# Position vectors as a bias row in the compression, GELU behind the transposes, and three query tiles split at full width and placed by DMA, in a hybrid attention block on Trainium2

## The chip, the cores and the metric

The kernel runs on one core of one Trainium2 chip (trn2). The metric is the device time of one launch in microseconds (us), lower is better. Before the change three timed runs gave 637.34, 634.45 and 636.11 us, with a median of 636.11 us. TensorE multiplies matrices, VectorE (DVE in the profile) and ScalarE (ACT) work element by element, GpSimd (POOL) does the same more slowly, and SyncE (SP) issues every DMA transfer, in order, from one queue.

## The reference, cut to what matters

The block has 512 tokens of width 1024. One input projection feeds a sparse attention group of 8 query heads in 2 key/value groups and a short convolution group; an output projection and a gated MLP follow. The part that the change touches is the compression of keys and values: windows of 32 tokens, one every 16 tokens (31 windows), get a position vector added to each token, go through a hidden layer of 256 with GELU, and become one compressed key or value each.

```python
def compress_kv(kv, pe, w1, w2):
    n_cmp = (S - L_CMP) // S_CMP + 1                       # 31
    idx = jnp.arange(n_cmp)[:, None] * S_CMP + jnp.arange(L_CMP)[None, :]
    blk = kv[:, idx] + pe[None, None, :, None, :]
    blk = blk.transpose(0, 3, 1, 2, 4).reshape(B, G, n_cmp, L_CMP * dh)
    return jax.nn.gelu(blk @ w1, approximate=True) @ w2
```

The queries are scaled by 1/8 and multiplied with compressed, selected and sliding-window keys. With these shapes the selected and the sliding branch both see all causal keys.

## The kernel before, in words

Every float32 operand is split into hi (the leading 12 bits, made by ScalarE as a copy into the type fp32r) and lo (the rest, made by VectorE as a subtraction). A projection is then three TensorE products per contraction tile of 128: weight hi with activation hi (L167), weight hi with activation lo (L168), weight lo with activation hi (L169), each 128x512. Weights come through `Stream`: SyncE loads a tile into one of 3 raw buffers (L72), ScalarE makes its hi part (L84), VectorE its lo part (L85; GpSimd for the eight tiles `w_c` of the compression's hidden layer), into a ring of 4 tiles. A raw buffer is loaded again when its lo part has been made.

The order of work: value and gate columns first; then the projections k0, k1 (keys), c0 (keys to compress), q0, q1 (queries of heads 0 to 3); then the attention, tile of 128 queries by tile, last tile first, with the remaining products as fillers between its pieces. The fillers are listed in `ORDER`: c1 (values to compress), q2, q3, the hidden layer h0 to h7, the second layer s, and then the convolution's products g, x, b. A scheduler (the tile framework) fixes the instruction order of each engine at build time by priorities; on the chip each engine then runs its own list in order, and an instruction whose operand is late holds all that stand behind it.

What the change touches:

- `queries(qa, p)` (L390 to L399) takes the projection `p` of two heads, multiplies it by the inverse norm (`normed`, L372, VectorE) into `qt`, and splits it head by head into `Q2`: ScalarE writes hi for 64 partitions (L397), VectorE writes lo into the other 64 partitions (L398). This is four instructions of 64x512 per query tile.
- `blocks(kv, p)` (L407 to L420) normalizes c0 or c1 into `ct`, and adds the position vectors `peT` while it gathers the windows: eight VectorE additions of 64x248 (L417) into two tiles `x`, each of which is then split into `X` (L420: ScalarE hi, VectorE lo, 128x496). The hidden layer's products `ph` (L441) take `X` as the stationary operand; one window slot of 32 in each group is a spare, set to zero.
- `second_layer()` (L445 to L472) adds the hi and lo rows of `ph` into `g1` (L450, L451), takes the GELU of them on ScalarE (L452), transposes (`pg`, L455), copies to `GT` and `GV` (L459, L461), and makes the compressed keys `KC` (L464 to L466, with a DMA that copies them to the other 64 partitions) and values `VC`.

The attention's scores are `sc` (L593); VectorE adds the bias and takes the minimum (L597, tile `P`), ScalarE the exponential (L599), VectorE makes the scale (`sums`, L604, L606), ScalarE (L613) or GpSimd (L611, the first head) multiplies by it, TensorE transposes (`tr`, L622), the result is split into `pth` and `ptl` (two buffers each, L131 and L132 in `split`), and multiplied with V into `o` (L630, L631). The compressed scores are `pcs` (L547).

Of the kernel before, what the change touches and what calls it, by code (L numbers as in the profile page):

```python
# [21 lines left out]
F32 = mybir.dt.float32  # L22
F32R = mybir.dt.float32r
# [7 lines left out]
NT = S // P          # token tiles  # L31
KT = D // P          # contraction tiles of the model width
# [9 lines left out]
# the projections and the first layer of the compression as they fill the gaps of the attention:  # L42
# values to compress c1, queries q, hidden layer h, second layer s, then gate g, input x, output gate b
# [3 lines left out]
T_TILES = 20         # kc vc ks kw q0-3 then (c x b) x 4  # L47
WARM = 8             # products on zeros while the first loads are under way


def f32(ap):
    return ap.bitcast(F32)


class Stream:
    """The dense weights in the order of their use: loaded some tiles ahead, split fewer ahead."""

    def __init__(self, tc, nc, raw, ring, items, loads=3, splits=2):
        self.tc, self.nc, self.raw, self.ring, self.items = tc, nc, raw, ring, items
        self.loads, self.splits = loads, splits  # L60
        self.raws, self.tiles = [], []
        self.at = 0
        self.early = False     # whether the splits go before what was emitted shortly before them
        self.pool_lo = set()  # tiles whose lo part GpSimd makes
        self.pieces = {}     # tiles that are split in pieces of so many columns
        self.other = {}      # tiles that go to another pool than the ring
# [41 lines left out]
def block_kernel(ctx: ExitStack, tc: tile.TileContext, a, out):  # L108
# [20 lines left out]
    def split(hi, lo, src):  # L129
        """hi = src rounded to 12 significant bits, lo = src - hi (exact)."""  # L130
        act(hi, src, AF.Copy)  # L131
        nc.vector.tensor_tensor(lo, src, f32(hi), op=ALU.subtract)  # L132

    VK = [0, 2, 5, KT]       # the k tiles of the value columns, as they share a tile of the ring
# [58 lines left out]
    # the tensor engine's clock comes up while the first loads are under way  # L193
# [6 lines left out]
    # bias tables: U[p, h, u] = -(bias of distance p + 384 - u), +BIG where it is negative  # L200
    # row r of vrows is the whole of vd; reading with a pitch one short shifts it by r
# [46 lines left out]
    def rstd_of(ss, name):  # L248
        """1 / rms of a row from the two halves of its mean square."""
# [21 lines left out]
    # The mean square of a row divides what comes out of the products, not what goes in.  # L271
    R = const.tile([P, 2, NT], F32, name="R")        # 1 / rms and its negative, by token
    Rb = ph1.tile([P, S], F32, name="Rb")            # the same, by token along the row
# [114 lines left out]
    # queries, scaled by -1/8; even heads keep hi in the low half, odd heads in the high half  # L388
    Q2 = r16("Q2", F32R).rearrange("p (h t) -> p h t", h=NH)

    def queries(qa, p):
        p = normed(p, f"qt{qa}")
        for e in range(2):
# [9 lines left out]
    # X[(l parity, d), l // 2, k/v, hi/lo, (group, block)] = kv + pe, the blocks padded to 32  # L403
    X = opool.tile([P, 16, 2, 2, NG, 32], F32R, tag="o16", name="X")
    nc.vector.memset(f32(X[:, :, :, :, :, NCMP:]), 0.0)

    def blocks(kv, p):  # L407
        p = normed(p, f"ct{kv}")
        for lh in range(2):
            x32 = ph1.tile([P, 8, NG, 32], F32, tag="t2", bufs=3, name=f"x32_{kv}_{lh}")  # L410
            for lp in range(2):
                for g in range(NG):
                    src = p[g * HD:(g + 1) * HD, :]
                    v = bass.AP(tensor=src.tensor, offset=src.offset + lp + 16 * lh,
                                ap=[src.ap[0], [2, 8], [16, NCMP]])
                    pev = peT[lp * HD:(lp + 1) * HD, kv, lh * 8:lh * 8 + 8]
                    nc.vector.tensor_tensor(  # L417
                        x32[lp * HD:(lp + 1) * HD, :, g, :NCMP], v,
                        pev[:, :, None].to_broadcast([HD, 8, NCMP]), op=ALU.add)
            ls = slice(lh * 8, lh * 8 + 8)  # L420
            split(X[:, ls, kv, 0, :, :NCMP], X[:, ls, kv, 1, :, :NCMP], x32[:, :, :, :NCMP])
# [7 lines left out]
    def hidden_steps(c):  # L429
        """First layer of the compression; rows 0-63 from X hi, rows 64-127 from X lo."""  # L430
# [3 lines left out]
        for l in range(2):  # L434
            l2 = 2 * c + l
            for kv in range(2):
                xs = X[:, l2, kv].rearrange("p s g n -> p (s g n)")
                for s in range(2):
                    cc = slice(l * 512 + kv * 256, l * 512 + kv * 256 + 256)
                    # one group over the bank: its first product opens it  # L440
# [4 lines left out]
    def second_layer():  # L445
        w2 = ph1.tile([P, 2, 2, HD], F32, tag="gz", bufs=1, name="w2")     # (half, k/v)
# [5 lines left out]
        act(g1[:HD, :S], g1[:HD, :S], AF.Gelu_apprx_tanh)  # L452
# [3 lines left out]
        GT = ph1.tile([P, 2, HD], F32, tag="t2", bufs=3, name="GT")  # L456
        GV = ph1.tile([P, 2, NG, 4, 32], F32, tag="t2", bufs=3, name="GV")
        pgv = pg[:, :256].rearrange("p (v f c) -> p v f c", v=2, f=2)
        nc.vector.tensor_copy(GT, pgv[:, 0])  # L459
        for g in range(NG):  # L460
            nc.vector.tensor_copy(GV[:, :, g], pgv[:, 1, :, None, 32 * g:32 * g + 32].to_broadcast([P, 2, 4, 32]))  # L461
        pc = pt_bank("pc")
        for hf in range(2):
            MM(pc[:HD, :HD], w2[:, hf, 0, :], GT[:, hf, :], start=hf == 0, stop=hf == 1)  # L464
# [109 lines left out]
    class Part:  # L574
        """Four heads of a group on a tile of queries: one branch, or both for the first tile."""
# [76 lines left out]
    def finish(o, i, g):  # L652
        # rows 0-63: V hi . P, rows 64-127: V lo . P
# [23 lines left out]
    for n, (i, g, bs) in enumerate(parts):  # L677
# [6 lines left out]
        # the share that goes between this part's pieces  # L684
# [45 lines left out]
    def token_major(w_tiles, ys, acts, on_half, on_tile, order):  # L730
        """The last products of a streamed contraction, one token tile after another."""
# [206 lines left out]
```

## Time and profile before

| what | value |
|---|---|
| timed runs | 637.34, 634.45, 636.11 us; median 636.11 us |
| span of the profiled execution | 633.9 us (the profile gives no other time for it) |
| TensorE busy | 617.5 us (97% of the span) |
| VectorE busy | 382.2 us (60%) |
| ScalarE busy | 306.5 us (48%) |
| GpSimd busy | 62.7 us (10%) |
| mean granted TensorE clock | 0.995 of full |

The span runs from the first to the last instruction; the lowest timed run is 0.55 us above it, the median 2.2 us. "Busy" is the share of time in which an engine has an instruction under way. Since TensorE is busy for nearly the whole span, a change helps only where it takes away one of TensorE's few waits, and costs where it makes a new one.

### The profile page before, as it was taken

Reading aid. Unit: us, or ns where it says so; the run is one execution under the profiler, and the core shown is the slowest. Engines: PE = TensorE matmul, PEld = TensorE weight load, DVE = VectorE, ACT = ScalarE, POOL = GpSimd, SP = SyncE. Lnnn points to the kernel's source line nnn. Section 1 sums busy time; section 2 is a strip of 40 time slices with the busy share of each in tenths; the row PEclk is TensorE's granted clock in tenths of the full one; section 3 lists DMA queues with packets and bytes.
Section 4 is the critical chain, followed back from the end, with each engine's and each line's share of the span. In section 5 each row is a group of like instructions: output and inputs, shape, how many; then the busy total and the mean of one; then the engine's idle time right before and its main releaser. Section 6 shows DMA issues by size and latency. Waiting matters only on the chain.

```text
span 633.9 us, 8027 instructions
## 1 busy us (share of the span) xinstructions
PE 617.5 (97%) x2980; PEld 511.3 (81%) x2980; DVE 382.2 (60%) x668; ACT 306.5 (48%) x556; POOL 62.7 (10%) x88
## 2 busy tenths in 40 slices
PE   8998899999999999999999999999999999999995
PEld 6886688887778788898888888888888888888884
DVE  5379967898988756648666656565656542222225
ACT  6546765798878644426443434444344422222212
POOL 1102453002130202200000000000000000000001
PEclk9999899999999999999999999999999999999999
DMA  8993355201121483004222233232322232232203
GB/s 293 329 304 129 133 180 189 74 10 43 42 78 53 169 280 130 8 5 143 93 96 98 99 100 101 100 100 99 101 87 95 89 114 87 94 100 99 67 0 133
DMA packets 25302, 72.00 MB, mean 114 GB/s; under 512 B 3136, under 2 KB 7048, under 8 KB 25008
## 3 DMA queue, kind: packets, MB, share of 16 engines
q1 hardware_dynamic: 25264, 71.50, 33.9%
q8 instruction: 23, 0.38, 0.2%
q14 instruction: 15, 0.12, 0.1%
HBM read 67.50 MB, written 4.74 MB: 114 GB/s over the span
## 4 chain that ended last, share of the span: by engine, by line
PE 80%; DVE 10%; DMA 3%; ACT 3%; issue 2%; POOL 1%; SPq 0%; DVEq 0%; POOLq 0%; ACTq 0%
PE pu L168 13%; PE pu L169 13%; PE pu L167 13%; PE z L743 6%; PE z L742 6%; PE z L744 6%; PE y L744 2%; PE y L743 2%; PE y L742 2%; DVE x L417 2%; DMA raw_q<-in_w_t 2%; PE tr L622 2%; PE sc L593 2%; PE o L631 1%; PE o L630 1%
## 5 line engine op out<-in xcount | busy, mean ns | idle before, releaser
L167 PE MATMUL pu<-h2T,w_u 128*128 128x512 f32 (+1 forms) x384 | 142.8, 372 | 0.0
L168 PE MATMUL pu<-h2T,w_u 128*128 128x512 f32 (+1 forms) x384 | 142.7, 372 | 0.0
L169 PE MATMUL pu<-h2T,w_u 128*128 128x512 f32 (+1 forms) x384 | 142.6, 371 | 0.0
L167 PEld LDWEIGHTS pu<-h2T,w_u 128*128 128x128 f32 x384 | 72.3, 188 | 12.6
L168 PEld LDWEIGHTS pu<-h2T,w_u 128*128 128x128 f32 x384 | 72.3, 188 | 12.6 <-DVE h2T L132 0.2
L169 PEld LDWEIGHTS pu<-h2T,w_u 128*128 128x128 f32 x384 | 72.3, 188 | 12.4
L826 DVE SCALAR_TENSOR_TENSOR cv<-pu,ffnw,cv 128x511 f32<-128x511 f32 x44 | 32.9, 749 | 70.2 <-ACT cv L825 70.2
L85 DVE TENSOR_TENSOR w_d<-raw_d,w_d 128x1024 fp32r<-128x1024 f32 x22 | 26.9, 1224 | 72.8 <-ACT w_d L84 72.8
L742 PE MATMUL z<-w_d,aT 128*128 128x512 f32 x176 | 68.5, 389 | 0.0
L743 PE MATMUL z<-w_d,aT 128*128 128x512 f32 x176 | 68.5, 389 | 0.0
L744 PE MATMUL z<-w_d,aT 128*128 128x512 f32 x176 | 68.5, 389 | 0.0
L825 ACT ACTIVATE cv<-pu,ffnw 128x512 f32<-128x512 f32 x44 | 30.3, 688 | 64.0 <-PE pu L169 63.9
L84 ACT ACTIVATE w_d<-raw_d 128x1024 fp32r<-128x1024 f32 x22 | 23.3, 1059 | 75.2 <-PE z L744 75.2
L85 DVE TENSOR_TENSOR w_u<-raw_u,w_u 128x1024 fp32r<-128x1024 f32 x44 | 53.4, 1217 | 5.9 <-ACT w_u L84 5.8
L84 ACT ACTIVATE w_u<-raw_u 128x1024 fp32r<-128x1024 f32 x44 | 46.2, 1052 | 6.6 <-PE pu L169 6.3
L599 ACT ACTIVATE P<-P,mins 128x512 f32<-128x512 f32 (+3 forms) x64 | 35.4, 554 | 11.5 <-DVE mins L597 11.1
L742 PEld LDWEIGHTS z<-w_d,aT 128*128 128x128 f32 x176 | 33.0, 188 | 6.9
L744 PEld LDWEIGHTS z<-w_d,aT 128*128 128x128 f32 x176 | 33.0, 188 | 6.9
L743 PEld LDWEIGHTS z<-w_d,aT 128*128 128x128 f32 x176 | 33.0, 188 | 6.7
L131 ACT ACTIVATE aT<-cv 128x512 fp32r<-128x512 f32 x22 | 13.9, 632 | 49.5 <-DVE cv L843 49.5
L251 POOL TENSOR_SCALAR rsz<-ssz 128x1 f32<-128x1 f32 x4 | 1.2, 300 | 355.2 <-ACT jz L865 355.2
L827 DVE SCALAR_TENSOR_TENSOR cv<-pu,ffnw,cv 128x510 f32<-128x510 f32 x44 | 32.8, 748 | 1.5
(215 smaller groups left out, 1158.7 us busy)
## 6 DMA issues: line engine op xcount, KB each, us to landing
raw_u<-in_w_u SPq DMA_DIRECT2D x44, 512.0 KB, 3.3
raw_d<-in_w_d SPq DMA_DIRECT2D x22, 512.0 KB, 3.2
raw_c<-in_w_c SPq DMA_DIRECT2D x8, 512.0 KB, 3.3
raw_o<-in_w_o SPq DMA_DIRECT2D x8, 512.0 KB, 3.4
vrows<-vd SPq DMA_DIRECT2D x2, 1280.0 KB, 10.4
xT<-in_xT SPq DMA_DIRECT2D x8, 256.0 KB, 5.3
xt<-in_x SPq DMA_DIRECT2D x4, 512.0 KB, 7.1
raw_q<-in_w_t SPq DMA_DIRECT2D x4, 512.0 KB, 7.0
```

The source lines that it names most:

```text
L84: self.nc.scalar.activation(t[:, 0, cs], self.raws[n][:, cs], AF.Copy)
L85: eng.tensor_tensor(t[:, 1, cs], self.raws[n][:, cs], f32(t[:, 0, cs]), op=ALU.subtract)
L167: MM(dst, wh, xh, start=first, stop=False)
L168: MM(dst, wh, xl, start=False, stop=False)
L169: MM(dst, wl, xh, start=False, stop=last)
L599: act(v, v, AF.Exp, bias=m, scale=-1.0, accum_out=self.sums[:, r, b:b + 1])
L742: MM(y, oh_, w[:, 0, cs], start=first, stop=False)
L743: MM(y, ol_, w[:, 0, cs], start=False, stop=False)
L744: MM(y, oh_, w[:, 1, cs], start=False, stop=last)
L825: act(t, pu, AF.Copy, scale=ffnw[:, m, 2:3])
L826: nc.vector.scalar_tensor_tensor(t[:, 1:], pu[:, :S - 1], ffnw[:, m, 1:2], t[:, 1:], op0=ALU.mult, op1=ALU.add)
L827: nc.vector.scalar_tensor_tensor(t[:, 2:], pu[:, :S - 2], ffnw[:, m, 0:1], t[:, 2:], op0=ALU.mult, op1=ALU.add)
```

## The change: what it does

- The position vectors are no longer added to the windows. By linearity they go through the hidden layer on their own: they are split once into the spare window slot of group 0 of `X`, so that their hidden row comes out of the same products; behind the transposes it is a column per hidden unit (`peb`), and ScalarE adds it as the bias of the GELU. The spare columns of `GT` are set to zero.
- `blocks` therefore splits the whole normalized projection once at 128x512 (`ch`, `cl`) and gathers the windows by eight copies of 64x496 elements that read every 16th element, four on ScalarE (hi) and four on VectorE (lo).
- The GELU moves from before the transposes (one instruction of 64x512) to behind them (four of 128x62, out of PSUM).
- Query tiles 0, 2 and 3 are split at 128x512 into `qh` and `ql` (in the buffers of `pth` and `ptl`), and four DMAs of 64x512 place them into `Q2`. Query tile 1 stays as it was.

All other lines of the difference remove comments.

```diff
     def queries(qa, p):
         p = normed(p, f"qt{qa}")
+        if qa != 1:
+            h_ = ph1.tile([P, S], F32R, tag="pth", bufs=2, name=f"qh{qa}")
+            l_ = ph1.tile([P, S], F32R, tag="ptl", bufs=2, name=f"ql{qa}")
+            act(h_, p, AF.Copy, scale=-0.125)
+            nc.vector.scalar_tensor_tensor(l_, p, -0.125, f32(h_), op0=ALU.mult, op1=ALU.subtract)
+            for e in range(2):
+                own = slice(e * HD, (e + 1) * HD)
+                oth = slice((1 - e) * HD, (2 - e) * HD)
+                nc.sync.dma_start(f32(Q2[own, 2 * qa + e, :]), f32(h_[own, :]))
+                nc.sync.dma_start(f32(Q2[oth, 2 * qa + e, :]), f32(l_[own, :]))
+            return
...
+    pe_lv = peT.rearrange("p v l -> p l v")
+    split(X[:, :, :, 0, 0, NCMP], X[:, :, :, 1, 0, NCMP], pe_lv)
     def blocks(kv, p):
         p = normed(p, f"ct{kv}")
-        for lh in range(2):
-            x32 = ph1.tile([P, 8, NG, 32], F32, tag="t2", bufs=3, name=f"x32_{kv}_{lh}")
-            for lp in range(2):
-                for g in range(NG):
...
-                    nc.vector.tensor_tensor(
-                        x32[lp * HD:(lp + 1) * HD, :, g, :NCMP], v,
-                        pev[:, :, None].to_broadcast([HD, 8, NCMP]), op=ALU.add)
-            ls = slice(lh * 8, lh * 8 + 8)
-            split(X[:, ls, kv, 0, :, :NCMP], X[:, ls, kv, 1, :, :NCMP], x32[:, :, :, :NCMP])
+        h_ = ph1.tile([P, S], F32R, tag="pth", bufs=2, name=f"ch{kv}")
+        l_ = ph1.tile([P, S], F32R, tag="ptl", bufs=2, name=f"cl{kv}")
+        split(h_, l_, p)
+        for lp in range(2):
+            for g in range(NG):
+                for s in range(2):
+                    src = (h_, l_)[s][g * HD:(g + 1) * HD, :]
+                    v = bass.AP(tensor=src.tensor, offset=src.offset + lp, ap=[src.ap[0], [2, 16], [16, NCMP]])
+                    dst = X[lp * HD:(lp + 1) * HD, :, kv, s, g, :NCMP]
+                    if s:
+                        nc.vector.tensor_copy(dst, f32(v))
+                    else:
+                        act(dst, f32(v), AF.Copy)
...
-        act(g1[:HD, :S], g1[:HD, :S], AF.Gelu_apprx_tanh)
...
+        GT = ph1.tile([P, 4, NG, 32], F32, tag="t2", bufs=3, name="GT")
+        peb = const.tile([P, 4], F32, name="peb")
+        pgv = pg[:, :256].rearrange("p (f g n) -> p f g n", f=4, g=NG)
+        nc.vector.tensor_copy(peb, pgv[:, :, 0, NCMP])
+        nc.gpsimd.memset(GT[:, :, :, NCMP:], 0.0)
+        for f in range(4):
+            act(GT[:, f, :, :NCMP], pgv[:, f, :, :NCMP], AF.Gelu_apprx_tanh, bias=peb[:, f:f + 1])
         for g in range(NG):
-            nc.vector.tensor_copy(GV[:, :, g], pgv[:, 1, :, None, 32 * g:32 * g + 32].to_broadcast([P, 2, 4, 32]))
+            nc.vector.tensor_copy(GV[:, :, g], GT[:, 2:, g, None, :].to_broadcast([P, 2, 4, 32]))
```

The scheduler then orders the engines' lists anew. In the lists below a row is an instruction with its line, its operation, and the tiles it writes and reads; the numbers are those of the buffers, and lines of the changed kernel are higher by up to 18.

VectorE of the kernel before, at the values' blocks (c1), where the scores' minima (`P`, shown as ISA) and the `sums` stand among the additions L417:

```order
L604 RECIPROCAL sums_560<-sums_560 128x2
L606 TENSOR_TENSOR sums_560<-sums_560,G 128x2
L85 TENSOR_TENSOR w_q_523<-raw_q_486,w_q_523 128x1024
L372 TENSOR_TENSOR ct_626<-pp_c_596,Rb 128x512
L597 ISA P_662,mins_595<-sc_661,U 128x512
L597 ISA mins_595 128x1
L417 TENSOR_TENSOR x_1_0_628<-ct_626,peT 64x8x31 x2
L604 RECIPROCAL sums_560<-sums_560 128x2
L417 TENSOR_TENSOR x_1_0_628<-ct_626,peT 64x8x31
L606 TENSOR_TENSOR sums_560<-sums_560,G 128x2
```

VectorE of the changed kernel at the same place:

```order
L410 SCALAR_TENSOR_TENSOR Q_460<-qt_556,Q_460 64x512 x2
L372 TENSOR_TENSOR ct_630<-pp_c_600,Rb 128x512
L85 TENSOR_TENSOR w_q_527<-raw_q_486,w_q_527 128x1024
L132 TENSOR_TENSOR cl_633<-ct_630,ch_632 128x512
L433 CAST X<-cl_633 64x16x31 x4
L615 ISA P_567,mins_565<-sc_566,U 128x512
L615 ISA mins_565 128x1
L615 ISA P_573,mins_565<-sc_572,U 128x512
L615 ISA mins_565 128x1
```

The normalization of c1 and its copies now stand ahead of the first head's score, and the lo part of q2's weights (`w_q_527`) stands behind the normalization of c1.

TensorE of the kernel before, where q2's projection (`pp_q_642`) begins:

```order
L593 MATMUL sc_661<-KK,Q_460 128x512
L167 MATMUL pp_q_642<-hT,w_q_523 128x512
L168 MATMUL pp_q_642<-hT,w_q_523 128x512
L593 MATMUL sc_661<-KK,Q_460 128x512
L622 MATMUL tr_681<-ident,P_563 128x128
L441 MATMUL ph<-w_c_0_597,X 128x256
L593 MATMUL sc_696<-KK,Q_460 128x512
L169 MATMUL pp_q_642<-hT,w_q_523 128x512
```

TensorE of the changed kernel from the tenth product of q2's projection (`pp_q_644`) on:

```order
L167 MATMUL pp_q_644<-hT,w_q_527 128x512
L168 MATMUL pp_q_644<-hT,w_q_527 128x512
L169 MATMUL pp_q_644<-hT,w_q_527 128x512
L455 MATMUL ph<-w_c_0_601,X 128x256 x2
L611 MATMUL sc_566<-KK,Q_460 128x512 x2
L167 MATMUL pp_q_644<-hT,w_q_527 128x512
L168 MATMUL pp_q_644<-hT,w_q_527 128x512
L455 MATMUL ph<-w_c_0_601,X 128x256 x6
L611 MATMUL sc_572<-KK,Q_460 128x512 x2
L611 MATMUL sc_582<-KK,Q_460 128x512 x2
L169 MATMUL pp_q_644<-hT,w_q_527 128x512
```

The scores stood among the products of c1 before; now c1's 24 products and q2's first twelve run ahead of the first score, and the hidden layer's first eight products (two, then six) stand around it.

SyncE of the changed kernel, where the placements of query tiles 2 (`qh_725`, `ql_726`) and 3 (`qh_835`, `ql_836`) stand among the weight loads (before, the same loads stood in the same order with nothing between them):

```order
L72 DMA raw_c_4_736<-in_w_c 128x1024
L72 DMA raw_c_5_750<-in_w_c 128x1024
L402 DMA Q_460<-qh_725 64x512
L403 DMA Q_460<-ql_726 64x512
L402 DMA Q_460<-qh_725 64x512
L403 DMA Q_460<-ql_726 64x512
L72 DMA raw_tx_784<-in_w_t 128x1024
L72 DMA raw_c_6_846<-in_w_c 128x1024
L402 DMA Q_460<-qh_835 64x512
L403 DMA Q_460<-ql_836 64x512
L402 DMA Q_460<-qh_835 64x512
L403 DMA Q_460<-ql_836 64x512
```

Behind these four stand the loads of `raw_c_7` and of the gate weights.

## Rows read from the trace of the kernel before

**Rows 1.** Busy time by stretch: start and end, length, then each engine; PEclk.

```profile
39.00:52.00 13.00, 13.00 (x59) 10.78 (x58) 12.59 (x26) 4.82 (x9) 0.00 (x0) 1.00 1.08 281
52.00:72.00 20.00, 15.27 (x62) 11.10 (x62) 19.30 (x33) 13.23 (x25) 6.54 (x3) 0.91 0.25 80
72.00:111.00 39.00, 38.58 (x212) 32.11 (x210) 28.61 (x40) 25.72 (x37) 20.17 (x11) 1.00 0.54 177
111.00:225.00 114.00, 111.99 (x592) 89.77 (x592) 95.58 (x296) 92.67 (x239) 19.03 (x28) 1.00 0.23 76
```

**Rows 2.** Timeline of TensorE, 50 to 72 us: start, length, instruction, [idle before, releaser].

```profile
50.01 0.39 PE L168 MATMUL pp_c<-hT,w_c 128*128 128x512 f32 x1
...
53.37 1.47 PE L593 MATMUL sc<-KK,Q 128*128 128x512 f32 x4 [0.93 <-issue]
...
60.54 0.33 PE L622 MATMUL tr<-ident,P 128*128 128x128 f32 x1 [0.78 <-POOL P L611]
...
67.60 0.45 PE L622 MATMUL tr<-ident,P 128*128 128x128 f32 x1 [2.96 <-ACT P L613]
...
70.20 0.63 PE L169 MATMUL pp_q<-hT,w_q 128*128 128x512 f32 x1
70.63 0.61 PE L167 MATMUL pp_q<-hT,w_q 128*128 128x512 f32 x1
```

**Rows 3.** Timeline of VectorE in the same stretch.

```profile
58.70 1.23 DVE L85 TENSOR_TENSOR w_q<-raw_q,w_q 128x1024 fp32r<-128x1024 f32 x1
...
61.04 4.74 DVE L417 TENSOR_TENSOR x<-ct,peT 64x248 f32<-64x248 f32 x2
...
66.57 0.16 DVE L606 TENSOR_TENSOR sums<-sums,G 128x2 f32<-128x2 f32 x1
```

**Rows 4.** Timeline of GpSimd in the same stretch.

```profile
60.45 4.97 POOL L85 TENSOR_TENSOR w_c<-raw_c,w_c 128x1024 fp32r<-128x1024 f32 x2
```

**Rows 5.** Groups of VectorE, 36 to 111 us: count | busy us, mean ns | idle before.

```profile
L417 DVE TENSOR_TENSOR x<-ct,peT 64x248 f32<-64x248 f32 x16 | 12.7, 795 | 0.3
L398 DVE SCALAR_TENSOR_TENSOR Q<-qt,Q 64x512 fp32r<-64x512 f32 x8 | 8.3, 1032 | 2.0 <-ACT Q L397 1.7
...
L372 DVE TENSOR_TENSOR qt<-pp_q,Rb 128x512 f32<-128x512 f32 x4 | 2.6, 682 | 0.0
L132 DVE TENSOR_TENSOR X<-x,X 128x496 fp32r<-128x496 f32 x4 | 2.6, 669 | 0.1
```

**Rows 6.** Groups of ScalarE, 36 to 111 us.

```profile
L84 ACT ACTIVATE w_c<-raw_c 128x1024 fp32r<-128x1024 f32 x9 | 9.5, 1055 | 3.4 <-PE pcg L169 1.6 <-issue 1.6 <-PE pp_q L169 0.2
...
L397 ACT ACTIVATE Q<-qt 64x512 fp32r<-64x512 f32 x8 | 5.0, 626 | 0.3 <-DVE qt L372 0.2
...
L131 ACT ACTIVATE X<-x 128x496 fp32r<-128x496 f32 x4 | 2.5, 616 | 7.4 <-DVE x L417 7.4
...
L353 ACT ACTIVATE ge<-pv,R 128x24 f32<-128x24 f32 x4 | 1.0, 278 | 0.7 <-DVE ge L354 0.7
```

**Rows 7.** Timeline of VectorE: single instructions with a strided and a contiguous source.

```profile
50.06 0.58 DVE L417 TENSOR_TENSOR x<-ct,peT 64x248 f32<-64x248 f32 x1
...
115.05 0.41 DVE L563 TENSOR_TENSOR zc<-zc,cm 128x248 f32<-128x248 f32 x1
```

**Rows 8.** DMA issues: count, KB each, median us from issue to landing.

```profile
KK<-KK SPq DMA_DIRECT2D x4, 256.0 KB, 6.6
...
KC<-KC SPq DMA_DIRECT2D x1, 32.0 KB, 3.0
...
peT<-in_pe SPq DMA_DIRECT2D x1, 16.0 KB, 9.6
```

**Rows 9.** Timeline of SyncE's queue: the placements of one compressed tile.

```profile
119.37 2.66 SPq L645 DMA_DIRECT2D bd<-zt  x4
```

**Rows 10.** Timelines of ScalarE and of TensorE's weight loads at the second layer.

```profile
102.20 0.60 ACT L450 ACTIVATE g<-ph 64x512 f32<-64x512 f32 x1
...
111.24 0.97 PEld L547 LDWEIGHTS pcs<-KC,Q 128*128 128x128 f32 x8 [0.51 <-DMA KC<-KC]
```

More of the change, by code (lines that the diff above doesn't have):

```diff
@@ L405, in block_kernel @@
     nc.vector.memset(f32(X[:, :, :, :, :, NCMP:]), 0.0)
+    pe_lv = peT.rearrange("p v l -> p l v")
+    split(X[:, :, :, 0, 0, NCMP], X[:, :, :, 1, 0, NCMP], pe_lv)
     def blocks(kv, p):
         p = normed(p, f"ct{kv}")
-        for lh in range(2):
-            x32 = ph1.tile([P, 8, NG, 32], F32, tag="t2", bufs=3, name=f"x32_{kv}_{lh}")
-            for lp in range(2):
-                for g in range(NG):
[L413 to L416, printed above, removed]
-                    nc.vector.tensor_tensor(
-                        x32[lp * HD:(lp + 1) * HD, :, g, :NCMP], v,
-                        pev[:, :, None].to_broadcast([HD, 8, NCMP]), op=ALU.add)
-            ls = slice(lh * 8, lh * 8 + 8)
-            split(X[:, ls, kv, 0, :, :NCMP], X[:, ls, kv, 1, :, :NCMP], x32[:, :, :, :NCMP])
+        h_ = ph1.tile([P, S], F32R, tag="pth", bufs=2, name=f"ch{kv}")
[11 more added lines that the diff above has]
+                        act(dst, f32(v), AF.Copy)
     blocks(0, pc0)
@@ L455, in second_layer @@
             nc.tensor.transpose(pg[:, n * HD:(n + 1) * HD], g1[:HD, n * P:(n + 1) * P], ident[:HD, :HD])
-        GT = ph1.tile([P, 2, HD], F32, tag="t2", bufs=3, name="GT")
+        GT = ph1.tile([P, 4, NG, 32], F32, tag="t2", bufs=3, name="GT")
         GV = ph1.tile([P, 2, NG, 4, 32], F32, tag="t2", bufs=3, name="GV")
-        pgv = pg[:, :256].rearrange("p (v f c) -> p v f c", v=2, f=2)
-        nc.vector.tensor_copy(GT, pgv[:, 0])
+        peb = const.tile([P, 4], F32, name="peb")
[4 more added lines that the diff above has]
+            act(GT[:, f, :, :NCMP], pgv[:, f, :, :NCMP], AF.Gelu_apprx_tanh, bias=peb[:, f:f + 1])
         for g in range(NG):
-            nc.vector.tensor_copy(GV[:, :, g], pgv[:, 1, :, None, 32 * g:32 * g + 32].to_broadcast([P, 2, 4, 32]))
+            nc.vector.tensor_copy(GV[:, :, g], GT[:, 2:, g, None, :].to_broadcast([P, 2, 4, 32]))
         pc = pt_bank("pc")
         for hf in range(2):
-            MM(pc[:HD, :HD], w2[:, hf, 0, :], GT[:, hf, :], start=hf == 0, stop=hf == 1)
+            MM(pc[:HD, :HD], w2[:, hf, 0, :], GT[:, hf].rearrange("p g n -> p (g n)"), start=hf == 0, stop=hf == 1)
         split(KC[:HD, 0], KC[:HD, 1], pc[:HD, :HD].rearrange("p (g n) -> p g n", g=NG))
```

## The prediction

> **What bounds the kernel now.** I read the table of busy time by stretch first. The reader is to see that TensorE is busy without a break up to 52 us, that it is idle for 20.00 - 15.27 = 4.7 us between 52 and 72 us, for 0.4 us between 72 and 111 us and for 2.0 us between 111 and 225 us [rows 1]. So TensorE sets the end, and there is one stretch of 20 us in which it waits. In the same stretch VectorE is busy for 19.30 of 20 us: TensorE waits for what VectorE has not yet got to.
>
> TensorE's timeline names the waits: 0.93 us ahead of the first scores, 0.78 us for a head scaled by GpSimd, 2.96 us for heads scaled by ScalarE [rows 2]; they sum to 4.67 us, nearly all of the 4.7. Behind the last of them a product begins 0.43 us after the one before, against 13.00 / 59 = 0.22 us in the full stretch before it [rows 1, 2]: that is the lower of the two clock levels, 1.2 GHz instead of 2.4. The mean granted clock of the stretch is 0.91, so the clock costs (1 - 0.91) x 20 = 1.8 us. Together the stretch loses 4.7 + 1.8 = 6.5 us, and this is what the change can give back there; with the 0.4 and 2.0 us of the next two stretches the most that could come back is 8.9 us.
>
> VectorE's timeline says why the longest wait is there: two of c1's additions take 4.74 us, and the `sums` that ScalarE's scaling needs come only at 66.57 [rows 3]. Alone an addition takes 0.58 us [rows 7]; the two that take 2.37 us each run while GpSimd makes two lo parts, from 60.45 to 65.42 [rows 4].
>
> **What VectorE and ScalarE gain and pay.** Removed from VectorE: 16 additions (12.7 us), 4 lo parts of `X` (2.6 us) and 6 of the 8 query splits (6 x 1.03 = 6.2 us) [rows 5], 21.5 us. Added: 2 lo parts at 128x512 and 3 for the queries, at 0.68 us like the normalization of the same size [rows 5], 3.4 us, and 8 gathering copies of 64x496.
>
> No row shows such a copy. From below it is 0.67 us, the lo part of 128x496 with contiguous rows [rows 5]; from above 2 x 0.58 = 1.16 us, twice an addition of 248 elements with the same stride [rows 7]. The stride costs: 0.58 against 0.41 us for the same number of elements, 0.17 us per 248. I take 0.67 + 2 x 0.17 = 1.0 us. (The Trainium skill, SBUF — State Buffer, in the note on cachelines under Door 1: The DMA port swizzle, says that accesses that step to a new 16-byte line pay; the rows agree, 0.58 against 0.41.) So VectorE saves 21.5 - 3.4 - 8.2 = about 10 us, 9 to 13 by the bounds.
>
> ScalarE gives up 4 x 0.62 + 6 x 0.63 = 6.3 us and gets 5 x 0.60 for the full-width hi parts and 8 copies. From below a copy is 0.62 [rows 6], from above 1.16 as on VectorE; I take 0.62 + 2 x 0.17 = 0.96. So ScalarE pays 3.0 + 7.7 - 6.3 = 4.4 us more. It was busy for 13.23 of the 20 us [rows 1], so it has room, but its order now matters. The split of `peT` and `peb` are tiny, 0.2 to 0.3 us each (as the 0.28 us of a 128x24 [rows 6]), and hidden.
>
> **What the new order makes of the 20 us.** This is worked along the lists of the changed kernel. c1's second product begins at 50.01 [rows 2]; 23 products of 0.23 us take it to 55.3, seen by VectorE at 55.5.
> - First wait. Normalization of c1 0.68 and the lo part of q2's weights 1.23 [rows 3] stand on VectorE one behind the other: 57.4. TensorE has two of q2's products before it needs that lo part, to 55.8: it waits 1.6 us. This wait does not hang on any unknown cost.
> - Second wait. ScalarE makes `ch` (0.6, to 56.8), one copy (0.96, 57.8), hi of `w_c_0` (1.06 [rows 6], 58.8), and GpSimd lo of it (4.97 / 2 = 2.5 [rows 4], 61.3). TensorE has ten products (2.3 us) and one hidden product, to 59.8: it waits 1.5 us. With copies of 0.62 it is 1.1.
> - Third wait. The next six hidden products need all copies of c1. ScalarE: second copy 59.8, hi of `w_c_1` 60.8, two copies 62.7. VectorE: `cl` 0.68 to 58.1, four copies to 62.2. TensorE is there at 62.3 and waits 0.4 us; with copies of 0.62 nothing.
> - The scores follow close behind each other, two score banks for six heads, and the first head still goes through GpSimd behind `w_c_1` (61.3 + 2.5 = 63.8). I put 0.3 us each for a bank and for that head, estimates from VectorE's 0.68 us per head against 0.46 us of score products.
>
> The sum is 1.6 + 1.5 + 0.4 + 0.6 = 4.1 us against 6.5: 2.4 us gained. No single wait reaches the 2.96 us after which the clock fell, so I take the full clock.
>
> **The placements.** Twelve DMAs of 64x512 are added, each issued in 2.66 / 4 = 0.66 us by SyncE [rows 9] and landing after 3.0 us (32 KB) to 6.6 us (256 KB) [rows 8]; I take 3.5, nearer the small one, since the 6.6 comes from a stretch with a DMA share of 1.08 and the placements go out at 0.25 to 0.54 [rows 1]. Those of tile 0 leave at about 52 to 54.5 and are needed by the score at 61.3: hidden even at 6.6. Tile 1 still splits in place. Those of tiles 2 and 3 stand in SyncE's queue behind loads that wait for GpSimd, and the gate loads stand behind them; I cost this at nothing, covered by the 20.17 us of GpSimd's work in 39 us that paces those loads anyway, and the rival below prices it.
>
> **The second layer.** GELU now stands between the transposes and the compressed keys: `peb` and four instructions of 0.28 us [rows 6], 1.4 us, longer by that than before, and the copies of `GT` go. TensorE had already waited 0.51 us for the DMA of the keys there [rows 10], and two products fewer cover it (0.45 us), so the bounds are 0 and 1.4 + 0.45 = 1.9 us. The transposes stand nine products earlier than before, 2.0 us, if `g` (0.60 us [rows 10]) is not late; I take 0.3 us, near the lower bound.
>
> **Sum.** 633.9 - 2.4 + 0.3 = 631.8 us of span. The lowest timed run is 0.55 us above the profiled span and the median 2.2 us, so on the scale of the median it is 634.0 us, 0.3% below 636.11.
>
> **The rivals.**
> - Cheap copies. At 0.62 us the second wait is 1.1, the third gone, and with scores that find their banks free 3.0 us remain: 3.5 gained, 3.8 without the loss in the second layer, 632.3 us. For it: contiguous rows at 0.62. Against: every strided row here is dearer.
> - The clock falls again. Between 55.8 and 62.7 TensorE idles 3.5 of 7 us. If that brings the lower level for as long as in [rows 2], 1.8 us go: 635.8 us. For it: the fall came behind idle time; against: each piece is shorter than 2.96.
> - Copies held by GpSimd. An addition took 2.37 instead of 0.58 us beside GpSimd [rows 3, 4, 7]. If copies are held the same way, the three that remain at 59.1 end at 61.5, 63.8 and 64.9, 2.2 us later than 62.7: 636.2 us. Against: the additions read two SBUF tiles, a copy one. The Trainium skill (SBUF — State Buffer, SBUF: two separate sides) describes the port that VectorE and GpSimd share as an exclusive lock, for VectorE's two-input instructions and for copies in a two-port mode; by that rule it depends on the mode, which no row shows.
> - Slower: the placements land late and hold ScalarE. `qh` of tile 3 takes a buffer that the placements of tile 2 must have read. These leave behind `raw_c_5`, at about 78 to 81 us; landing after 3.0 us they end near 84. `w_tx`, `w_c_6` and `w_c_7` stand on ScalarE behind `qh`, and `raw_c_7` on SyncE behind the placements of tile 3. I count a slack of 1.2 us at `w_c_7`, by TensorE's products up to it. At 6.6 us landing it all comes 3.6 us later and TensorE loses 2.4 us, just what was gained; at 9.6 us (the slowest row, 16 KB [rows 8]) 5.4 us: 634.0 + 5.4 = 639.4 us. It decides from about 6 us of landing on. For it: the 6.6 and the 9.6; against: the queues are emptier here.
>
> **How the numbers follow.** My forecast 0.46, with a range of its own of 632 to 636; cheap copies 0.20; the clock 0.12; held copies 0.08; late placements 0.14. A difference of 0.5%, 3.2 us, is about what a measurement of this kernel tells from none, as its three runs lie 2.9 us apart. Faster by more: 0.18 of my forecast (its lower end) and 0.18 of the cheap copies, 0.36. Slower by more: 0.13 of the late placements and 0.01 of the held copies, 0.14. Between: 0.50. The range that leaves two in ten out goes from 630.3 (all new waits near their lower ends) to 637.8 (placements somewhat late).
>
> **What would show it.** In the changed profile the additions L417 are gone and 8 copies L433 stand at 0.67 to 1.16 us; TensorE waits about 1.6 us for the lo part of `w_q` near 56 us and about 1.5 us for GpSimd's `w_c` near 60; no wait of about 3 us for a scaled head; idle time and clock loss from 52 to 72 us near 4 us instead of 6.5. It is wrong if copies beside GpSimd take over 2 us, if ScalarE waits for a DMA ahead of `qh` of tile 3 for more than 2 us, if a gate or `w_c` weight comes late between 85 and 100 us, or if the granted clock between 55 and 65 us falls below 0.9.

## The result, and the profile after

The changed kernel takes 639.26 us (median of 6 runs, 637.65 to 643.01) against 635.32 us for the kernel before in the same session (6 runs): ratio 1.0072, 95% interval 1.0044 to 1.0100. It is slower by 0.7%. Three of its six runs lie at 637.65 to 638.02 us and three at 640.51 to 643.01 us, and the profiled execution is the one of 640.51 us, so the waits and the clock below are those of one of the longer three. The profiled span is 638.7 us instead of 633.9.

Busy time by stretch of the changed kernel, with the columns of [rows 1]:

```profile
39.00:52.00 13.00, 13.00 (x59) 10.76 (x58) 10.31 (x21) 8.25 (x12) 0.00 (x0) 1.00 0.94 236
52.00:72.00 20.00, 15.03 (x55) 11.31 (x53) 14.93 (x26) 13.22 (x20) 5.79 (x3) 0.83 0.36 109
72.00:111.00 39.00, 36.00 (x182) 29.15 (x183) 24.55 (x31) 24.66 (x38) 19.31 (x12) 0.96 0.61 191
111.00:225.00 114.00, 112.50 (x603) 90.43 (x602) 94.49 (x295) 91.06 (x238) 19.05 (x28) 1.00 0.20 60
```

Read it as the prediction read [rows 1]: idle time of TensorE plus (1 - granted clock) times the stretch. From 52 to 72 us that is 5.0 + 3.4 = 8.4 us, where it was 6.5; from 72 to 111 us it is 3.0 + 1.6 = 4.6, where it was 0.4; from 111 to 225 us it is 1.5, where it was 2.0. The three sum to 14.5 against 8.9, 5.6 us more; the query products had started 0.6 us sooner (38.33 instead of 38.91 us), and the span is 4.8 us longer. So VectorE did get free time in the first stretch (14.93 us busy instead of 19.30), and the end of the kernel got none of it.

TensorE's timeline of the changed kernel shows four waits where [rows 2] had three:

```profile
56.73 0.50 PE L169 MATMUL pp_q<-hT,w_q 128*128 128x512 f32 x1 [1.46 <-DVE w_q L85]
60.87 0.39 PE L455 MATMUL ph<-w_c,X 128*128 128x256 f32 x1 [1.46 <-POOL w_c L85]
64.09 1.62 PE L455 MATMUL ph<-w_c,X 128*128 128x256 f32 x6 [1.91 <-DVE X L433]
67.22 0.63 PE L169 MATMUL pp_q<-hT,w_q 128*128 128x512 f32 x1
67.64 0.63 PE L167 MATMUL pp_q<-hT,w_q 128*128 128x512 f32 x1
...
107.59 0.69 PE L468 MATMUL pg<-ident,g 64*128 64x64 f32 x4 [2.50 <-DVE g L465]
108.20 0.79 PE L168 MATMUL pbg<-hT,w_tb 128*128 128x512 f32 x1
108.79 0.63 PE L169 MATMUL pbg<-hT,w_tb 128*128 128x512 f32 x1
109.22 0.63 PE L167 MATMUL pbg<-hT,w_tb 128*128 128x512 f32 x1
```

Behind the third and behind the fourth wait products begin 0.42 to 0.43 us apart (67.22 and 67.64, 108.79 and 109.22): the lower clock level, 1.2 GHz, twice. The wait of 2.96 us for a scaled head is gone, as forecast.

The third wait is explained by VectorE and GpSimd, the stretch of [rows 3, 4] in the changed kernel; the first line is the other block's copies, with GpSimd idle:

```profile
43.66 1.78 DVE L433 CAST X<-cl 64x496 fp32r<-64x496 f32 x3
...
57.31 6.63 DVE L433 CAST X<-cl 64x496 fp32r<-64x496 f32 x4
...
58.42 5.08 POOL L85 TENSOR_TENSOR w_c<-raw_c,w_c 128x1024 fp32r<-128x1024 f32 x2 [30.86 <-ACT w_c L84]
```

A copy alone takes 1.78 / 3 = 0.59 us. Four of them, with GpSimd's two lo parts beside them, take 6.63 instead of 2.4 us, and end 0.4 us after GpSimd does.

The fourth wait is explained by the queues. Here are SyncE's queue, VectorE, GpSimd and ScalarE of the changed kernel ahead of `pg`; they answer to [rows 8 to 10]:

```profile
87.97 2.41 POOL L85 TENSOR_TENSOR w_c<-raw_c,w_c 128x1024 fp32r<-128x1024 f32 x1 [0.62 <-ACT w_c L84]
...
88.86 2.06 DVE L398 SCALAR_TENSOR_TENSOR ql<-qt,qh 128x512 fp32r<-128x512 f32 x1 [1.19 <-ACT qh L397]
...
88.86 0.48 SPq L402 DMA_DIRECT2D Q<-qh  x1
90.95 0.46 SPq L403 DMA_DIRECT2D Q<-ql  x1
91.47 0.60 SPq L402 DMA_DIRECT2D Q<-qh  x1
92.12 0.59 SPq L403 DMA_DIRECT2D Q<-ql  x1
92.80 0.53 SPq L72 DMA_DIRECT2D raw_c<-in_w_c  x1
...
96.87 1.06 ACT L84 ACTIVATE w_c<-raw_c 128x1024 fp32r<-128x1024 f32 x1 [4.06 <-DMA raw_c<-in_w_c]
...
103.72 1.06 ACT L84 ACTIVATE w_tx<-raw_tx 128x1024 fp32r<-128x1024 f32 x1 [2.92 <-DMA raw_tx<-in_w_t]
104.80 0.59 ACT L464 ACTIVATE g<-ph 64x512 f32<-64x512 f32 x1
...
104.81 1.46 DVE L85 TENSOR_TENSOR w_tx<-raw_tx,w_tx 128x1024 fp32r<-128x1024 f32 x1 [1.58 <-ACT w_tx L84]
...
106.86 0.67 DVE L465 TENSOR_TENSOR g<-ph,g 64x512 f32<-64x512 f32 x1
```

`ql` of tile 3 takes 2.06 us, beside GpSimd's lo part, so its placement leaves at 90.95. `raw_c_7` stands behind it and is asked for at 92.80, though its buffer was free at 87.97 + 2.41 = 90.38. ScalarE waits 4.06 us for it, the next `w_tx` comes late behind that, and `g`, which stands on ScalarE behind `w_tx`, begins only at 104.80. VectorE's part of `g`, the one that `pg` waits for, stands behind the lo part of the same `w_tx` and begins at 106.86.

The groups of copies and full-width splits, 36 to 111 us, and the landing of the placements, against [rows 5, 6, 8]:

```profile
L433 DVE CAST X<-cl 64x496 fp32r<-64x496 f32 x8 | 9.0, 1120 | 0.1
L398 DVE SCALAR_TENSOR_TENSOR ql<-qt,qh 128x512 fp32r<-128x512 f32 x3 | 4.5, 1504 | 1.9 <-ACT qh L397 1.9
```

```profile
L435 ACT ACTIVATE X<-ch 64x496 fp32r<-64x496 f32 x8 | 8.5, 1068 | 0.1
```

```profile
Q<-qh SPq DMA_DIRECT2D x6, 128.0 KB, 4.2
Q<-ql SPq DMA_DIRECT2D x6, 128.0 KB, 4.0
```

The 1.12 us of VectorE's copies is a mean of two very different kinds, four at 0.6 us and four at 1.66. The placements land in 4.0 to 4.2 us.

### The profile page after: what moved, and what is told of

Its sections match the earlier page's. It is cut to its first block, busy times and chain, and to the rows that moved or that the text cites. A ratio compares the mean times of both kernels' runs of the same rounds, so it can differ in the third digit from the quotient of the medians.

```text
span 638.7 us, 8042 instructions
## 1 busy us (share of the span) xinstructions
PE 619.6 (97%) x2980; PEld 512.5 (80%) x2980; DVE 374.7 (59%) x656; ACT 311.8 (49%) x563; POOL 61.1 (10%) x89
## 3 DMA queue, kind: packets, MB, share of 16 engines
HBM read 67.50 MB, written 4.74 MB: 113 GB/s over the span
## 4 chain that ended last, share of the span: by engine, by line
PE 89%; DVE 3%; DMA 3%; ACT 1%; POOL 1%; issue 1%; SPq 1%; POOLq 0%; DVEq 0%; ACTq 0%
PE pu L169 13%; PE pu L168 13%; PE pu L167 13%; PE z L762 6%; PE z L761 6%; PE z L760 6%; PE sc L611 3%; PE tr L640 3%; PE y L762 2%; PE y L761 2%; PE y L760 2%; PE o L648 2%; PE o L649 1%; DVE X L433 1%; PE pcg L168 1%
## 5 line engine op out<-in xcount | busy, mean ns | idle before, releaser
L615 DVE CUSTOM_DVE_ANT_0 P<-sc,U 128x512 f32<-128x512 f32 (+3 forms) x64 | 30.3, 484 | 6.6 <-PE sc L611 5.6
```

The lines of the kernel that those rows point to most:

```text
L615: nc.vector.tensor_tensor_reduce(v, sc[:, b * nk:(b + 1) * nk], U[:, h, 384 - P * i:S], 1.0, 3e38, ALU.add, ALU.min, m)
```

## Experiments

Two theories. Theory 1: GpSimd's lo parts of `w_c_0` and `w_c_1` hold the copies of c1, and the new order, c1 whole ahead of the scores, puts them side by side. Theory 2: tile 3's placements, in SyncE's queue ahead of `raw_c_7`, make `g` late. Times are medians; the ratio is to the kernel before in the same session, with its 95% interval.

**Lo parts on VectorE.**

```diff
-    W.pool_lo |= {f"c1_{c}" for c in range(8)}
+    W.pool_lo |= {f"c1_{c}" for c in range(2, 8)}
```

> The changed kernel, with the lo parts of w_c_0 and w_c_1 made by VectorE instead of GpSimd; nothing runs on GpSimd beside the copies of c1's lo part any more. Theory 1 (the copies are held by GpSimd): each of the four copies takes 0.59 us as the three undisturbed ones do, against 6.63 us for four; with two lo parts of 1.21 us more on VectorE the first minimum of a score starts near 57.3 + 2.4 + 2.4 = 62.1 us instead of 64.0, the wait of the products with w_c_0 for GpSimd goes (1.6), and the clock may stay up between 64 and 70 us: 636.5 to 637.5 us. Rival (these copies are slow by themselves, since they read tile c1, or write partitions 64 to 127 from 0 to 63): they stay at 1.6 to 2.0 us, VectorE gets 2.4 us more to do in the same place, and the time is 640 to 642. The loss between 92 and 111 us stays in either case.

Measured 636.48 us, ratio 1.0017 (1.0001 to 1.0032), at the lower edge of what theory 1 gave. VectorE's copies of c1:

```profile
57.52 0.62 DVE L433 CAST X<-cl 64x496 fp32r<-64x496 f32 x1
58.58 1.23 DVE L85 TENSOR_TENSOR w_c<-raw_c,w_c 128x1024 fp32r<-128x1024 f32 x1 [0.43 <-ACT w_c L84]
59.84 0.62 DVE L433 CAST X<-cl 64x496 fp32r<-64x496 f32 x1
...
62.65 1.22 DVE L433 CAST X<-cl 64x496 fp32r<-64x496 f32 x2
```

Every copy takes 0.61 to 0.62 us, although VectorE makes 2.4 us of lo parts besides, and the clock is 1.00 from 52 to 72 us. Theory 1 holds, its rival falls. The wait at `pg` is still there, 2.27 us.

**Tile 3 in place, and the same on top of the lo parts on VectorE.** The condition says which tiles go by DMA:

```diff
-        if qa != 1:
+        if qa in (0, 2):
```

> The changed kernel, with query tile 3 split in place by halves as before the change; tiles 0 and 2 still go by DMA. The order up to 72 us is the same. Theory 2 (tile 3's four placements, which wait in SP's queue for the split of tile 3, keep raw_c_7 and behind it raw_tx from being asked for): raw_c_7 is issued near 90.4 us, when GpSimd has done with its buffer, instead of 92.8; g starts 2 us or more earlier, the 2.50 us in which the transpose pg waits go to under 1, the clock doesn't fall behind 108 us: 635.5 to 637 us. Rival (the GELU's move behind the transposes, or the loads' own landing of 4.0 us, makes that wait): pg still waits 2 us or more and the time stays at 638.5 to 640.

> The lo parts of w_c_0 and w_c_1 on VectorE (as in the run before that had this alone, at 636.48 us) and query tile 3 split in place, tiles 0 and 2 by DMA. Theory 2 (tile 3's placements hold raw_c_7 and raw_tx in SP's queue): the 2.3 us that the transpose pg waits for g go to 1.0 or less, and the time is 1 to 2 us under that run: 634.5 to 635.5. Rival (what the in-place split of tile 3 adds on ScalarE and VectorE, 0.65 and 0.72 us, is late there instead, since the split weights and g stand behind it): 636 to 637.

Alone it measured 640.09 us, 1.0073 (1.0054 to 1.0092): no gain, against theory 2's 635.5 to 637. The wait at `pg` did shrink, from 2.50 to 1.09 us, and the clock stayed up behind it, but its profiled execution had lost 3.6 us before the first query product (last section), so its median can't settle what this is worth. Counted from the first query product to the end, that execution took 596.9 us, against 600.4 in the changed kernel and 595.0 in the kernel before: 3.5 us less. But 1.6 us of what it lost less is a clock that stayed low for a shorter time behind three waits of nearly the same lengths (0.91 instead of 0.83 in those 20 us), which the edit doesn't explain.

With the lo parts on VectorE the same edit measured 634.58 us, 0.9993 (0.9970 to 1.0016), 1.9 us under the run without it (0.24% by the ratios), with 1.06 us at `pg`. That is what theory 2 expected, but the two intervals overlap, and the two profiled executions take the same time (634.89 and 634.78 us): what `pg` no longer waits comes back as a wait of 1.31 us at 85 us, where it was 0.26. This pair alone doesn't show theory 2.

**Bias row alone, and with the lo parts on VectorE.** No tile is placed (`if qa > 9:`).

> The bias row, the copies and the GELU behind the transposes, with all four query tiles split in place by halves: no placement at all. Theories 1 and 2 together: the loss between 92 and 111 us (2.66 us of wait and about 1.5 of clock) goes, the copies of c1's lo part still stand beside GpSimd's two lo parts and take 1.6 to 2.0 us each: 635.5 to 637.5. If the whole loss came from the placements: 632 to 634.5. If it came from the bias row alone: 638.5 to 640.

> The bias row with no placements (635.06 us in its own run) and the lo parts of w_c_0 and w_c_1 on VectorE. There GpSimd's two lo parts held a 128x2 multiplication for 1.50 us instead of 0.16 and a 128x512 subtraction for 0.88 instead of 0.68. Theory 1: these go, VectorE gets 2.4 us of lo parts, which it has idle time for (2.0 us at 61.7): 633.5 to 635. Rival (VectorE is the bound from 57 to 72 us, so 2.4 us more of work cost more than 1.5 us of being held): 635.5 to 637.

The first measured 635.06 us, 1.0004 (0.9985 to 1.0024): the bias row, its copies and the later GELU cost nothing that can be measured, and the loss needs the placements. The time lies between what both theories together gave (635.5 to 637.5) and what the placements alone would (632 to 634.5). Its copies of c1 stand behind GpSimd's lo parts, and what stands beside them is held instead; VectorE, with GpSimd below:

```profile
56.48 0.16 DVE L624 TENSOR_TENSOR sums<-sums,G 128x2 f32<-128x2 f32 x1
...
60.04 0.16 DVE L622 RECIPROCAL sums<-sums 128x2 f32<-128x2 f32 x1
60.23 1.50 DVE L624 TENSOR_TENSOR sums<-sums,G 128x2 f32<-128x2 f32 x1
...
59.30 4.75 POOL L85 TENSOR_TENSOR w_c<-raw_c,w_c 128x1024 fp32r<-128x1024 f32 x2 [1.78 <-ACT w_c L84]
```

A multiplication of two SBUF tiles with two elements in each partition takes 1.50 us, where the same one takes 0.16 at 56.48 with GpSimd idle. The reciprocal, which has one input, is not held: it takes 0.16 us inside GpSimd's time. The second measured 633.79 us, 0.9980 (0.9962 to 0.9998), under both kernels, if only just. So 0.72% of loss became 0.17 without the hold, -0.07 with tile 3 in place too, and -0.20 with every tile in place; of these steps the first is clear of noise, and so are the other two taken together.

**The queries alone,** with the compression and second layer of the kernel before.

> The other half alone: the compression and its second layer as before the change, query tiles 0, 2 and 3 split at full width and placed by DMA. Theory 2: raw_c_7 is held by tile 3's placements here too, so a wait of about 2.5 us with some clock behind it stands near 107 us, and what ScalarE and VectorE are spared (4 x 0.63 + 4 x 1.03 less the full-width ones) gives little of it back: 636.5 to 639. Rival (placements are harmless, the bias row does all of it): 633 to 635.

Measured 644.17 us, 1.0142 (1.0123 to 1.0161), dearer than either theory said. One of c1's additions, ahead of the lo part of `w_q` on VectorE, is held for 2.27 us instead of 0.58; TensorE waits 3.8 us for `w_q`, 1.8 for `X` and 2.3 for `g`. Without the copies the new order meets the slower additions beside GpSimd.

**Single tiles by DMA.** `if qa in (2, 3):`, then `if qa == 0:`.

> The changed kernel with only query tile 0 placed by DMA, tiles 2 and 3 split in place; the lo parts stay on GpSimd. If the loss from 52 to 72 us comes from the placed tiles 2 or 3 (their earlier end draws the scores' order) it goes, and with tile 3's placements the wait at pg: 634 to 636. If it comes from tile 0 alone: the loss of 8.7 us (products spaced wider than at full clock, 52 to 72 us) stays, the copies still stand beside GpSimd's lo parts, and only the wait at pg shrinks: 637 to 639.

This expectation names the tiles the wrong way round: in the kernel that ran, tiles 2 and 3 went by DMA and tile 0 was split in place. It measured 639.08 us, 1.0051 (1.0027 to 1.0074). The clock stayed at 1.00 from 52 to 72 us, with 2.1 us idle, and the wait at `pg` was 2.4 us, with a lower clock behind it. The other way round, as meant:

> The changed kernel with query tile 0 placed by DMA and tiles 1, 2 and 3 in place (this is what the expectation of the earlier run said; that run had tile 0 in place and tiles 2 and 3 placed). VectorE's order up to 72 us is that of the changed kernel: c1's copies stand ahead of the scores, beside GpSimd's lo parts. If tile 0's placement alone brings this order and theory 1 is right, the four copies take 6 to 7 us, the loss from 52 to 72 us is 8 us or more, the wait at pg is about 1.1: 637.5 to 640. Rival (the loss needs tile 2's placements too): under 636.

Measured 638.97 us, 1.0053 (1.0037 to 1.0070). The four copies take 6.66 us, TensorE waits 1.46, 1.45 and 1.94 us and the clock is 0.91 from 52 to 72 us; at `pg` it waits 1.1. So tile 0's placement alone brings the order that theory 1 needs, and tile 3's the wait of theory 2. Each alone costs 0.5% where all three cost 0.72 (0.44 to 1.00), so the two losses may not add. Part of that stands in the traces: the order with tile 0 in place has a wait of its own, 1.70 us at 82.7 us, where the changed kernel waits 0.27. Whether this is all of it is open; `pg` waits about as long in both, 2.36 and 2.50 us.

**Tile 3 alone by DMA, then from ScalarE's queue.** Both with the lo parts on VectorE, so that they differ from the 633.79 us in tile 3 alone (`if qa == 3:`), and from each other in the queue:

```diff
-                nc.sync.dma_start(f32(Q2[own, 2 * qa + e, :]), f32(h_[own, :]))
-                nc.sync.dma_start(f32(Q2[oth, 2 * qa + e, :]), f32(l_[own, :]))
+                nc.scalar.dma_start(f32(Q2[own, 2 * qa + e, :]), f32(h_[own, :]))
+                nc.scalar.dma_start(f32(Q2[oth, 2 * qa + e, :]), f32(l_[own, :]))
```

> The bias row, the lo parts of w_c_0 and w_c_1 on VectorE, and query tile 3 alone placed by DMA; it differs from the run with all tiles in place (633.79 us) in tile 3 alone, and up to 83 us the order is the same. Theory 2: tile 3's four placements stand in SP's queue between raw_c_6 and raw_c_7, and go only when tile 3 is split; raw_c_7, raw_tb and raw_tg are asked for 1 to 3 us later, g with them, the wait at pg grows from 1.1 to 2.3 or more: 635 to 637 us, more where the clock falls behind that wait. Rival (tile 3's placements are harmless by themselves): the full-width split saves VectorE 0.7 us there and the time stays at 633.3 to 634.3.

> As the run with tile 3 alone placed by DMA (638.11 us), with its four placements issued from ScalarE's queue, between w_tx and w_c_6; VectorE's, GpSimd's and TensorE's orders are the same, and SP's list is the same without the four. Theory 2 (the place in SP's queue is what costs, not the transfers): raw_c_7 is asked for when GpSimd has done with its buffer, near 85.7 us instead of 88.56. ScalarE waits for ql (to 86.2) and pays four issues of some 0.5 us ahead of w_c_6, so that w_c_6 moves from 86.7 to about 88.4 and w_c_7 from 92.0 to about 90; the wait at pg falls from 2.9 to 1.5 us or less and the clock stays up behind it: 633.5 to 635.5 us. Rival (the transfers beside the loads, or the late split of tile 3, make the loads late whatever the queue): the wait at pg stays over 2 us and the time at 637 to 639.

From SyncE's queue: 638.11 us, 1.0047 (1.0027 to 1.0066), 4.3 us more than in place and above the 635 to 637 that theory 2 gave. GpSimd, VectorE, SyncE's queue, ScalarE and TensorE of that run:

```profile
83.29 2.41 POOL L85 TENSOR_TENSOR w_c<-raw_c,w_c 128x1024 fp32r<-128x1024 f32 x1 [2.44 <-ACT w_c L84]
...
83.76 2.48 DVE L398 SCALAR_TENSOR_TENSOR ql<-qt,qh 128x512 fp32r<-128x512 f32 x1 [1.73 <-ACT qh L397]
...
86.27 0.48 SPq L403 DMA_DIRECT2D Q<-ql  x1
...
88.56 0.33 SPq L72 DMA_DIRECT2D raw_c<-in_w_c  x1
...
92.00 1.06 ACT L84 ACTIVATE w_c<-raw_c 128x1024 fp32r<-128x1024 f32 x1 [4.21 <-DMA raw_c<-in_w_c]
...
103.59 0.46 PE L468 MATMUL pg<-ident,g 64*128 64x64 f32 x4 [2.88 <-DVE g L465]
```

The split is held as in the changed kernel, `raw_c_7` is asked for 2.9 us after its buffer is free (83.29 + 2.41 = 85.70), and `pg` waits 2.88 us. The placements themselves land in 2.3 to 2.6 us here. With every tile in place `raw_c_7` is asked for within 0.4 us of its buffer and `pg` waits 1.06.

From ScalarE's queue: 636.09 us, 1.0000 (0.9983 to 1.0017): 2.0 us less by the medians, 0.47% by the ratios. VectorE's and TensorE's orders are the same and `ql` is held as long; only the queue differs. SyncE, ScalarE's queue, ScalarE and TensorE:

```profile
80.62 5.20 SPq L72 DMA_DIRECT2D raw_c<-in_w_c  x2
...
86.05 0.47 ACTq L403 DMA_DIRECT2D Q<-ql  x1
...
87.95 1.06 ACT L84 ACTIVATE w_c<-raw_c 128x1024 fp32r<-128x1024 f32 x1 [3.49 <-DVE w_tx L85]
...
93.25 1.06 ACT L84 ACTIVATE w_tb<-raw_tb 128x1024 fp32r<-128x1024 f32 x1 [2.47 <-DMA raw_tb<-in_w_t]
```

`raw_c_7` is now issued by 85.82, when its buffer is free. But ScalarE stands behind the held `ql` itself, `w_c_6` comes at 87.95, and `pg` still waits 1.9 us with a lower clock behind. So the place in SyncE's queue carries about half to two thirds of the price (2.0 of 4.3 us, or 0.47 of 0.67%, each difference known to some 0.26%). By the trace the rest moves to the engine that issues: `w_c_6` comes 1.2 us later than from SyncE's queue (87.95 against 86.72). Neither expectation held: theory 2 said 633.5 to 635.5, its rival 637 to 639, and the time fell between them.

**All placements from ScalarE's queue** (the same edit of the queue, in the changed kernel).

> The changed kernel with all twelve placements issued from ScalarE's queue instead of SP's. The scores now stand ahead of c1's copies on VectorE and TensorE. Theory 2: SP asks for raw_c_7 near 90.4 us again; ScalarE pays some 0.5 us for each placement, six us in all, of which the four of tile 3 lie ahead of w_c_7 and g: the wait at pg stays near 1.5 to 2.5. If c1's copies come after GpSimd's lo parts are done, each takes 0.59 us. 636 to 639 us. Rival (what matters is that the transfer lies between the split and the scores, whatever the queue): the scores of head 0 wait 2 us or more for Q and the time is 639 to 643.

Measured 637.13 us, 1.0023 (1.0004 to 1.0042), within the expectation: `pg` waits 1.1 us, three hidden products wait 2.4 us in all for GpSimd, and a score waits 1.9 us for the DMA of `Q`, the only trace here in which TensorE waits for a placement's landing.

**The kernel before, with the lo parts on VectorE.**

> The kernel before the change, with the lo parts of w_c_0 and w_c_1 on VectorE and nothing else changed. Theory 1 says that the hold is not the change's own: in the kernel before, two additions took 4.74 us beside GpSimd's two lo parts instead of 1.16. Without these lo parts on GpSimd every addition takes 0.58 us, the wait of 2.96 us for a scaled head goes or shrinks, and the clock stays up: 631 to 634 us. Rival (2.4 us of lo parts more on a VectorE that was busy for 19.3 of 20 us cost as much as the hold): 634.5 to 636.5.

Measured 635.51 us, 0.9997 (0.9979 to 1.0014): no change, as the rival said. The hold does go: six additions take 3.58 us, 0.60 each, and TensorE's idle time from 52 to 72 us falls from 4.7 to 2.4 us. But a wait of 1.4 us at 84 us is new, and the clock falls as before (0.91), now behind a single wait of 1.82 us. From the first query product to the end the profiled execution is 1.5 us shorter than that of the kernel before; that the lo parts on VectorE take the rest back is not shown.

## Why the prediction was wrong

- **First and second wait: right.** Forecast 1.6 and 1.5 us; the trace says 1.46 and 1.46 us of idle time, in the places named. The 0.6 us for score banks and the first head did not come: the three waits make 4.83 of 4.97 us of idle time.
- **Third wait: the step that failed first.** The term was 0.4 us, from copies at 1.0 us. Alone a copy takes 0.59 us, but beside GpSimd four took 6.63, and the wait was 1.91. Held copies were a rival at 0.08. The evidence for it stood in [rows 3, 4]: two additions in 4.74 us beside GpSimd. I set it aside because an addition reads two tiles of SBUF and a copy one. The Trainium skill, VectorE: DVE Perf Modes, section "Mode 2×_2P — use both read ports for one tensor", says that in this mode a copy from SBUF to SBUF reads its one source through both ports, two elements at a time. The trace agrees: 496 elements in 0.59 us, where an addition needs 0.58 for 248 [rows 7]. The Trainium skill, SBUF — State Buffer, section "SBUF: two separate sides", counts an instruction in such a mode among those that the lock holds, and the runs agree: 0.6 us without GpSimd, 1.7 on the mean with it. No row of before shows such a copy, so its speed could not give the mode away. The stride's price was taken rightly: 248 pairs at the speed of the strided addition are 0.58 us. What made 1.0 us of it was the 0.67 for one element at a time.
- **"I take the full clock": failed.** It rested on no single wait reaching 2.96 us. The clock fell at the end of three waits of 1.46, 1.46 and 1.91 us between 55 and 64 us. In other traces it fell behind a single wait of 1.82 (the kernel before with the lo parts on VectorE), 1.90 or 2.27 us (the queries alone), and did not behind one of 1.94 (all placements from ScalarE's queue) or 2.27 (lo parts on VectorE), so the length of one wait doesn't decide it. With the third wait this is what turned 4.1 us into 8.4. The rival that named it had the right stretch and half the price: 1.8 us against 3.4 in the profiled execution, though the same three waits cost just 1.8 in the runs with tile 3 in place and with tile 0 alone.
- **"I cost this at nothing" of tiles 2 and 3's placements: failed.** The cover named was GpSimd's pace, which the loads follow anyway. But the placements wait for tile 3's split, the split was held by GpSimd until its lo part ended, and so a load that should leave with the end of this lo part left after the four placements, 2.4 us later. That took 2.50 us and a clock fall. The late-placement rival had this place, `raw_c_7` behind tile 3's placements, but tied it to landing times of 6 us and more; they were 4.0 to 4.2, and with tile 3 alone 2.3 to 2.6 at the same lateness of the load. The queue's order was the mechanism, and a `ql` that took 2.06 us, where [rows 5] give 0.68 for the same size, part of the price.
- **ScalarE's copies** took 1.07 us, where 0.96 was taken; near the upper bound of 1.16, and it cost nothing that the runs could show. **The second layer** was put at 0.3 us; the bias row with the GELU behind the transposes came out at 1.0004.
- The sum of 634.0 us is 0.8% low: of 5.6 us lost more than before, 4.2 stand at `raw_c_7` and `g`, in a stretch that the sum left out, and 1.9 from 52 to 72 us where it had 2.4 of gain (the last stretch gave 0.5 back).

## What to carry to other kernels

When a row shows an instruction of VectorE four times too long beside GpSimd, treat every copy and every operation on two SBUF tiles that the change moves into GpSimd's time as held, a tiny one too, until a run shows otherwise. A DMA added to a queue of loads is priced by what it waits for and by the load behind it, not by its landing time. Several waits that are each too short to matter can still bring the clock down together.

## What the hardware showed beside that

The length of a hold doesn't go by the size: 128x2 took 1.50 us. It goes by what is left of GpSimd's instruction: `ql` ended 0.54 us behind it in the changed kernel (90.92 against 90.38) and in the run with tile 3 alone (86.24 against 85.70). Operations that read one of two tiles out of PSUM were not held: inside GpSimd's lo parts a score's minimum took 0.68 us (bias row alone, at 59.43) and `ptl` 0.69 (tile 3 alone, at 78.86). A copy of stride 64 bytes at the source runs at two elements in the time of one on VectorE (0.59 us for 496, where the strided addition takes 0.58 for 248), while the same copy takes 1.07 us on ScalarE, against 0.62 for contiguous rows [rows 6]. And the start of the first query product differs by up to 3.8 us between the profiled executions (38.14 to 41.95 us), though TensorE has the same products before it. In the one with tile 3 in place a load of 1 KB landed 0.5 us later, and TensorE, after a wait, began at the lower clock; its first products, and the same place in the changed kernel:

```profile
9.79 1.81 PE L284 MATMUL pb<-oh,relT 32*8 32x512 f32 x2 [2.12 <-DMA relT<-in_relT]
...
11.93 0.43 PE L298 MATMUL pv<-w_v,hT 128*128 128x280 f32 x1
12.16 0.43 PE L299 MATMUL pv<-w_v,hT 128*128 128x280 f32 x1
```

```profile
9.27 1.01 PE L284 MATMUL pb<-oh,relT 32*8 32x512 f32 x2 [0.99 <-DMA relT<-in_relT]
...
10.45 0.29 PE L298 MATMUL pv<-w_v,hT 128*128 128x280 f32 x1
10.58 0.29 PE L299 MATMUL pv<-w_v,hT 128*128 128x280 f32 x1
```

Products follow each other by 0.23 us in the one and 0.13 in the other, and the queries' first product begins at 41.95 instead of 38.33 us. Whether this is what spreads the runs of one kernel by some 3 us is not shown; where it matters, the traces are compared above from the query products on.
